# Twelve adaLN reductions taken out of the first FFN and placed in the mixer, eleven of them from the keys' projection on

## The chip, the core and the metric

The kernel is one launch on one core of a Trainium2 chip (trn2). The metric is device time in microseconds (us), taken as the median of several runs. All sizes are float32: one layer of a model of width 2048, 256 tokens, batch 1. The engines are called as the profile calls them: PE (TensorE, matrix products), PEld (its weight loads), DVE (VectorE), ACT (ScalarE), POOL (GpSimd) and SP (SyncE, which here only issues the large DMA transfers).

## The reference, cut to what matters

The layer is two half-step feed-forward blocks (FFN) around a mixer. Each of the three sublayers is modulated: its input is shifted and scaled, and its output is gated, by vectors that come from one large matrix `w_ada` and a single conditioning vector `c`.

```python
mod = (jax.nn.silu(c) @ w_ada[l] + b_ada[l]).reshape(B, N_SUBLAYERS, 3, D_MODEL)
shift, scale, gate = mod[:, :, 0], mod[:, :, 1], mod[:, :, 2]
y = _swiglu(modulate(x, 0), ffn1_w13[l], ffn1_w2[l])
x = _layer_norm(ALPHA * x + FFN_WEIGHT * gate[:, 0, None, :] * y, ln_g[l, 0], ln_b[l, 0])
proj = modulate(x, 1) @ w_in[l] + b_in[l]
q, k, v, o, i_pre, f_pre, x_rg, g_rg = jnp.split(proj, ...)
...                                   # mLSTM heads on q, k, v; RG-LRU on x_rg, g_rg
y = jnp.concatenate([h_m, h_r], axis=-1) @ w_out[l]
x = _layer_norm(ALPHA * x + gate[:, 1, None, :] * y, ln_g[l, 1], ln_b[l, 1])
y = _swiglu(modulate(x, 2), ffn2_w13[l], ffn2_w2[l])
x = _layer_norm(ALPHA * x + FFN_WEIGHT * gate[:, 2, None, :] * y, ln_g[l, 2], ln_b[l, 2])
```

`silu(c) @ w_ada` has 3 x 3 x 2048 outputs, and each is a dot product of length 2048. These outputs are the "adaLN tiles" of the title: 128 outputs to a tile, 144 tiles. They depend on `c` alone, so that a tile can be computed at any time before the sublayer that uses it.

## The kernel before, in words

**Weights.** All weights are read once, in tiles of 128 x 2048 float32 (1 MB each). `load` (line 77) takes a buffer with `raw_tile` (line 68, four buffers in all, one tag "raw") and issues the transfer on SP's queue. `split` (line 84) makes two halves of a tile for PE: ACT casts it to a rounded high part (line 91), DVE subtracts that from the raw tile to give the low part (line 93). High and low parts have three buffers each ("hi" and "lo"). Each product is then taken as high x high, low x high and high x low: lines 252 to 254 in `mov_t` and lines 241 and 243 in `stat_u`. In the profile's names a raw tile begins with r, its high part with h and its low part with l: `rs`, `hs`, `ls` belong to one tile of the `w_s` projections, `rv`, `hv`, `lv` to the values, `rwo`, `hwo`, `lwo` to the output projection, `rw`, `rfg` and `rfv` to the FFNs.

**adaLN tiles.** `ada_tile` (line 166) takes the next tile of the list `todo`, loads it into one of the same four raw buffers, and lets DVE reduce it against a broadcast of silu(c) in one instruction (line 175), with a short instruction behind it that writes the 128 sums. PE and ACT have no part in it. The tiles are spread by a credit: each `load` calls `tick` (line 183), which adds a rate to a counter and issues one adaLN tile for each whole unit:

```python
credit[0] += credit[1]
while todo and credit[0] >= 1.0:
    credit[0] -= 1.0
    ada_tile()
```

The rate is set at the beginning of each stage: `RAMP_RATE` for the first five stages, `FFN1_RATE` at line 835, `MIX_RATE` at line 933 in `mixer`, `FFN2_RATE` at line 839. `ada_until` (line 178) issues in one go what a stage needs and hasn't got yet; with the rates before and after the change only line 1162 may find anything left to do.

**PSUM.** All products go to eight banks of 128 x 512 float32 (`bank`, line 65). A bank is free again when its last reader on ACT or DVE is done.

**Order.** The instructions of a stage are written in program order, but a scheduler of the framework sets the order on each engine from its own estimate of the times, and it also decides which buffer and which bank a tile takes. On the chip each engine then works through its own list strictly in that order and waits on semaphores. So a change in the number of DVE instructions changes all engines' lists.

**The mixer** (line 899), in the order of its program: the output gate's projection; the input and forget gates; eight tiles for the RG-LRU's input (line 1045) with the convolution; eight for its gelu gate (line 1049) with the recurrence (line 1013) and `rg_out` (line 1030, DVE instructions on 128 x 512); the values in two groups of four tiles, two banks per group (lines 1057 to 1067: the products go to `pv`, and DVE adds the bias and moves them out at line 1065); eight tiles of keys (line 1069: `pj`, moved out by ACT at line 916 and DVE at line 917); eight of queries, two to a head. Between the heads' queries PE takes up the attention of the heads before: `head` (line 1073) forms masks from `pm` on DVE (lines 1078 and 1080), ACT's exponential (line 1082), and the weighted scores from `pk` on DVE (line 1089, in place in `misc`); `head_out` (line 1092) multiplies them with the values into `pn` and normalises that on DVE and POOL (lines 1100 to 1115). The last two heads stand between the tiles of the output projection (`out_tile`, line 1132, products into `pw`); `head_split` (line 1117) transposes their results, and the mixer ends with a boundary that leads to the second FFN.

## Time and profile before

| | |
|---|---|
| median of 3 runs | 1914.12 us (1912.11 to 1915.27) |
| the profiled execution: its own time | 1910.49 us |
| the profiled execution: its span | 1908.7 us |
| DVE busy in the span | 1434.7 us (75%) |
| ACT busy in the span | 835.3 us (44%) |
| mean granted clock of PE | 0.996 |

The profiled execution is a fourth run beside the three; its span is counted from its first to its last instruction, and the 1.8 us between that and its own time lie around the span.

How the work lies in the span (a view by windows, DVE's adaLN instructions taken alone in the last column):

| stretch, us from the start | stage | PE busy | DVE busy | DMA rate | adaLN on DVE |
|---|---|---|---|---|---|
| 307 to 745 | first FFN behind the ramp | 435.31 of 438 | 364.68 | 350 GB/s | 140.72 us |
| 824 to 968 | mixer, RG-LRU and values | 143.69 of 144 | 137.12 | 291 GB/s | 30.36 us |
| 968 to 1035 | keys and the first queries | 67.00 of 67 | 52.72 | 309 GB/s | 14.15 us |
| 1035 to 1110 | heads and output projection | 75.00 of 75 | 60.37 | 231 GB/s | 14.06 us |

A row of the lists below reads: start or line, duration, engine, line of the kernel, operation, output and inputs, shape, and how many instructions are merged in it ("x4"); in brackets stands how long the engine was idle ahead of it and who ended that. A DVE instruction overlaps the next by a little, so that what it costs in a row of work is the distance from its start to the next one's. The clock is the share of full speed that was granted to PE in a window.

### The profile page before, as it was taken

To read this page: it belongs to the slowest core of one execution; us is meant where nothing else is said; L and a number is where in the kernel's file an instruction comes from. 1 tells how busy PE (TensorE), PEld (TensorE's weight loads), DVE (VectorE), ACT (ScalarE), POOL (GpSimd) and SP (SyncE) were. 2 spreads that over 40 slices of the span, in tenths; PEclk is the share of its full clock that TensorE was granted. 3 is DMA by queue.
4 is the path that set the end of the run, shared out by engine and by line. 5 is a ranking of instruction groups with operands and counts; after the bars stand their busy time and mean duration, and the time that the engine had idled before them with its cause. 6 is when DMAs were issued, how large, how long until landed. Compare 5 with 4: busy or idle time off the path is not lost.

```text
span 1908.7 us, 21186 instructions
## 1 busy us (share of the span) xinstructions
PE 1868.9 (98%) x8551; PEld 1543.8 (81%) x8551; DVE 1434.7 (75%) x1394; ACT 835.3 (44%) x788; POOL 39.5 (2%) x65
## 2 busy tenths in 40 slices
PE   6999999999999999999999999999999999999997
PEld 5778888888887888688888887888888888888886
DVE  7999898888887977889996887555555644545676
ACT  5434344533333335756644356443444333333341
POOL 0000000000000000100000121000000000000000
PEclk9999999999999999999999999999999999999999
DMA  9999888999999987477687563676666655555552
GB/s 370 345 344 346 319 301 346 348 364 359 346 353 358 354 326 264 151 271 293 252 321 288 207 260 131 241 264 224 261 240 247 240 195 182 196 193 205 198 220 88
DMA packets 73203, 515.88 MB, mean 270 GB/s; under 512 B 8544, under 2 KB 8720, under 8 KB 11024
## 3 DMA queue, kind: packets, MB, share of 16 engines
q1 hardware_dynamic: 70848, 507.54, 71.0%
q10 hardware_dynamic: 1728, 3.80, 0.6%
q0 software_dynamic: 528, 3.17, 0.4%
q8 instruction: 67, 1.10, 0.2%
q14 instruction: 32, 0.26, 0.0%
HBM read 512.36 MB, written 2.12 MB: 270 GB/s over the span
## 4 chain that ended last, share of the span: by engine, by line
PE 88%; DVE 5%; DMA 3%; ACT 2%; issue 2%; POOL 0%; DVEq 0%; ACTq 0%; POOLq 0%
PE py L253 6%; PE py L254 6%; PE py L252 6%; PE fg L253 6%; PE fg L254 6%; PE fg L252 6%; PE pj L241 5%; PE fv L253 5%; PE fv L254 5%; PE fv L252 5%; PE pj L243 3%; PE tl L252 2%; PE tl L253 2%; PE tl L254 2%; PE rg L685 2%
## 5 line engine op out<-in xcount | busy, mean ns | idle before, releaser
L175 DVE CUSTOM_DVE_ANT_0 ada<-ada,scb,badac 128x2048 f32<-128x2048 f32 x142 | 332.7, 2345 | 7.1 <-DMA ada<-in_w_ada 7.0
L93 DVE TENSOR_TENSOR lw<-rw,hw 128x2048 fp32r<-128x2048 f32 x81 | 185.2, 2288 | 96.8 <-ACT hw L91 96.8
L91 ACT CAST hw<-rw 128x2048 fp32r<-128x2048 f32 x81 | 155.0, 1913 | 226.3 <-PE py L254 68.1
L93 DVE TENSOR_TENSOR lfv<-rfv,hfv 128x2048 fp32r<-128x2048 f32 x60 | 137.5, 2292 | 129.5 <-ACT hfv L91 129.3
L93 DVE TENSOR_TENSOR lfg<-rfg,hfg 128x2048 fp32r<-128x2048 f32 x60 | 137.4, 2290 | 92.9 <-ACT hfg L91 92.9
L253 PE MATMUL py<-lw,hth 128*128 128x512 f32 x512 | 200.3, 391 | 2.6 <-DVE lw L93 2.5
L254 PE MATMUL py<-hw,htl 128*128 128x512 f32 x512 | 200.0, 391 | 0.0
L91 ACT CAST hfg<-rfg 128x2048 fp32r<-128x2048 f32 x60 | 114.9, 1915 | 190.3 <-PE fv L254 55.9
L252 PE MATMUL py<-hw,hth 128*128 128x512 f32 x512 | 196.9, 393 | 0.0
L253 PE MATMUL fg<-lfg,u 128*128 128x512 f32 x480 | 187.0, 389 | 0.1
L254 PE MATMUL fg<-hfg,u 128*128 128x512 f32 x480 | 187.0, 389 | 0.0
L253 PE MATMUL fv<-lfv,u 128*128 128x512 f32 x480 | 186.8, 389 | 0.0
L91 ACT CAST hfv<-rfv 128x2048 fp32r<-128x2048 f32 x60 | 114.7, 1912 | 164.5 <-PE fg L254 91.7
L254 PE MATMUL fv<-hfv,u 128*128 128x512 f32 x480 | 186.7, 389 | 0.0
L252 PE MATMUL fg<-hfg,u 128*128 128x512 f32 x480 | 185.0, 392 | 0.0
L252 PE MATMUL fv<-hfv,u 128*128 128x512 f32 x480 | 183.5, 389 | 0.0
L91 ACT CAST hra<-rra 128x2048 fp32r<-128x2048 f32 x47 | 89.9, 1915 | 133.6 <-PE rv L686 50.6
L241 PE MATMUL pj<-u,hs 128*128 128x512 f32 x512 | 122.5, 391 | 0.0
L253 PEld LDWEIGHTS py<-lw,hth 128*128 128x128 f32 x512 | 96.6, 189 | 23.6 <-DVE lw L93 3.9
L93 DVE TENSOR_TENSOR lra<-rra,hra 128x2048 fp32r<-128x2048 f32 x47 | 107.3, 2285 | 9.3 <-ACT hra L91 9.1
L254 PEld LDWEIGHTS py<-hw,htl 128*128 128x128 f32 x512 | 96.5, 189 | 20.1
L252 PEld LDWEIGHTS py<-hw,hth 128*128 128x128 f32 x512 | 96.1, 188 | 19.5
(445 smaller groups left out, 3470.7 us busy)
## 6 DMA issues: line engine op xcount, KB each, us to landing
ada<-in_w_ada SPq DMA_DIRECT2D x144, 1024.0 KB, 5.5
rw<-in_w SPq DMA_DIRECT2D x81, 1024.0 KB, 4.9
rfg<-in_w SPq DMA_DIRECT2D x60, 1024.0 KB, 4.9
rfv<-in_w SPq DMA_DIRECT2D x60, 1024.0 KB, 4.8
rra<-in_w_r SPq DMA_DIRECT2D x48, 1024.0 KB, 5.5
rs<-in_w_s SPq DMA_DIRECT2D x32, 1024.0 KB, 4.8
rwo<-in_w_out SPq DMA_DIRECT2D x16, 1024.0 KB, 4.8
rv<-in_w_vo SPq DMA_DIRECT2D x8, 1024.0 KB, 4.9
```

Of the source, the lines that this page charges most:

```text
L91: act.copy(cut(hi, w), like(raw[:, w], hi))
L93: low.tensor_sub(cut(lo, w), like(raw[:, w], lo), cut(hi, w).bitcast(F32))
L175: vec.tensor_tensor_reduce(raw[:, c], raw[:, c], scb[:, c], 1.0, base, ALU.mult, ALU.add, to)
L241: nc.tensor.matmul(ps, hi[:, k * P:(k + 1) * P], both(k), start=k == 0, stop=False)
L243: nc.tensor.matmul(ps[:, 0:S], lo[:, k * P:(k + 1) * P], uh[:, k, :], start=False, stop=k == KT - 1)
L252: nc.tensor.matmul(o, acth[:, k0 + j, tk], cut(hi, w), start=first and j == 0, stop=False)
L253: nc.tensor.matmul(o, acth[:, k0 + j, tk], cut(lo, w), start=False, stop=False)
L254: end = nc.tensor.matmul(o, actl[:, k0 + j, tk], cut(hi, w), start=False, stop=last and j == 3)
L685: nc.tensor.matmul(pss[t], uh[:, k0 + j, tk], lo[:, w], start=False, stop=False)
```

## The change

Two rates change, and one of them gets a second value that holds from the keys' projection on.

```diff
-FFN1_RATE = 0.88
-MIX_RATE = 0.5
+FFN1_RATE = 0.72
+MIX_RATE = (0.55, 1.05)
...
-                credit[:] = -2.0, MIX_RATE
+                credit[:] = -2.0, MIX_RATE[0]
...
         kt_ = v8(slot("k"))
+        credit[1] = MIX_RATE[1]
         proj(17, 8, kt_)
```

No instruction is added or removed; 144 adaLN tiles are issued as before. Counted in SP's list of transfers:

| stage | loads of weights | adaLN tiles before | after |
|---|---|---|---|
| ramp | | 40 | 40 |
| first FFN behind it | 72 | 63 | 51 |
| mixer, up to the keys | | 11 | 12 |
| mixer, from the keys on | 24 that may bring one | 14 | 25 |
| second FFN | | 16 | 16 |

The scheduler then orders all lists anew from the first FFN on. From line 1069 on, line numbers of the kernel are higher by one after the change (DVE's line 1089 is 1090, and so on). Three places are shown.

**DVE, behind the values and ahead of line 1065.** The L1065 rows move the values out of their four banks; L93 on `ls` is the low part of a tile of the keys, L175 an adaLN reduction, the `t`, `rl` rows the end of `rg_out`. Before, with the third tile of the keys (`ls_6870`) just ahead of the four rows:

```order
L175 ISA ada_6908,adac<-ada_6908,scb,badac 128x2048
L175 ISA adac 128x1
L1040 SCALAR_TENSOR_TENSOR t_6490<-t_6490,xc 128x512
L1037 TENSOR_TENSOR t_6499<-t_6499,gg 128x512
L93 TENSOR_TENSOR ls_6829<-rs_6826,hs_6828 128x2048
L1042 TENSOR_TENSOR rl<-t_6490,rh 128x512
L1039 SCALAR_TENSOR_TENSOR t_6499<-t_6499,gg 128x512
L93 TENSOR_TENSOR ls_6870<-rs_6867,hs_6869 128x2048
L1040 SCALAR_TENSOR_TENSOR t_6499<-t_6499,xc 128x512
L1065 TENSOR_TENSOR v<-pv_6515,bv_6517 128x2x256
L1065 TENSOR_TENSOR v<-pv_6516,bv_6517 128x2x256
```

After it, with the sixth tile of the keys (`ls_6975`) ahead of them:

```order
L93 TENSOR_TENSOR ls_6931<-rs_6928,hs_6930 128x2048
L175 ISA ada_6969,adac<-ada_6969,scb,badac 128x2048
L175 ISA adac 128x1
L1039 SCALAR_TENSOR_TENSOR t_6463<-t_6463,gg 128x512
L1042 TENSOR_TENSOR rl<-t_6454,rh 128x512
L93 TENSOR_TENSOR ls_6975<-rs_6972,hs_6974 128x2048
L175 ISA ada_7013,adac<-ada_7013,scb,badac 128x2048
L175 ISA adac 128x1
L1040 SCALAR_TENSOR_TENSOR t_6463<-t_6463,xc 128x512
L1065 TENSOR_TENSOR v<-pv_6479,bv_6481 128x2x256
L1065 TENSOR_TENSOR v<-pv_6480,bv_6481 128x2x256
```

Between the low part of the last gelu-gate tile (line 93, `ls_6433` before and `ls_6397` after) and the first L1065 row, DVE's list has 12 rows of line 93 and 5 adaLN reductions before, and 15 and 10 after.

**PE, the fourth, fifth and sixth tile of the keys**, with the semaphores that a row waits for. Before:

```order
L241 MATMUL pj_6907<-u_105,hs_6913 128x512 [waits Activation_49]
L241 MATMUL pj_6907<-u_105,hs_6913 128x512 x15
L243 MATMUL pj_6907<-u_105,ls_6914 128x256 [waits DVE_49]
L243 MATMUL pj_6907<-u_105,ls_6914 128x256 x15
L241 MATMUL pj_6951<-u_105,hs_6954 128x512 [waits Activation_49]
L241 MATMUL pj_6951<-u_105,hs_6954 128x512 x15
```

After:

```order
L241 MATMUL pj_6880<-u_105,hs_6886 128x512 [waits Activation_49]
L241 MATMUL pj_6880<-u_105,hs_6886 128x512 x15
L243 MATMUL pj_6880<-u_105,ls_6887 128x256 [waits DVE_49]
L243 MATMUL pj_6880<-u_105,ls_6887 128x256 x15
L241 MATMUL pj_6924<-u_105,hs_6930 128x512 [waits DVE_49,Activation_49]
L241 MATMUL pj_6924<-u_105,hs_6930 128x512 x15
```

The fifth tile's product (`pj_6924`) now waits for DVE ahead of its first matmul: the value of that semaphore in the built program is the one that the first L1065 row raises, since the tile takes the bank of `pv_6479`. The sixth to eighth tile wait in the same way for the other three L1065 rows.

**PE, the last two heads** (`pn_7700` before, `pn_7697` after is the first product of head 3 with the values, `pn_7614` and `pn_7633` are those of head 2; `pm` and `pk` are head 3's mask and scores; `pw` is the output projection). Before, right behind head 2's two products:

```order
L1077 MATMUL pm_7656<-misc,ident 128x256
L1085 MATMUL pk_7661<-qt_7449,k 128x256 x2
L1087 MATMUL pk_7661<-qt_7449,k 128x128 x2
L253 MATMUL pw_7586<-lwo_7673,rh 128x512
L254 MATMUL pw_7586<-hwo_7672,rl 128x512
L252 MATMUL pw_7586<-hwo_7672,rh 128x512
L253 MATMUL pw_7586<-lwo_7673,rh 128x512
L254 MATMUL pw_7586<-hwo_7672,rl 128x512
L252 MATMUL pw_7586<-hwo_7672,rh 128x512
L253 MATMUL pw_7586<-lwo_7673,rh 128x512
L254 MATMUL pw_7586<-hwo_7672,rl 128x512
L1097 MATMUL pn_7700<-v,misc 128x257
```

After:

```order
L1098 MATMUL pn_7614<-v,misc 128x257
L1098 MATMUL pn_7633<-v,misc 128x257 x2
L1078 MATMUL pm_7653<-misc,ident 128x256
L1086 MATMUL pk_7658<-qt_7440,k 128x256 x2
L1088 MATMUL pk_7658<-qt_7440,k 128x128 x2
L1098 MATMUL pn_7697<-v,misc 128x257
L1098 MATMUL pn_7716<-v,misc 128x257 x2
L252 MATMUL pw_7736<-hwo_7743,rh 128x512
```

Before, eight matmuls of the output projection stand between head 3's scores and its product with the values; after it they stand ahead of `pn_7614`, and none is left between. `pn_7697` waits for the last of these DVE rows, which follow in DVE's list after the change upon line 1101 of `pn_7633`:

```order
L175 ISA ada_7865,adac<-ada_7865,scb,badac 128x2048
L175 ISA adac 128x1
L1079 SCALAR_TENSOR_TENSOR misc<-pm_7653,gcol,misc 128x256
L1081 SCALAR_TENSOR_TENSOR misc<-pm_7653,gcol,misc 128x128
L93 TENSOR_TENSOR lwo_7838<-rwo_7835,hwo_7837 128x2048
L1103 TENSOR_TENSOR rd_7616<-rd_7616,pn_7614 128x1
L1115 TENSOR_SCALAR pn_7529<-pn_7529,hmv_7537,rsh_7543 128x256
L1106 BN_STATS hst_7620<-pn_7614 128x6
L1103 TENSOR_TENSOR rd_7636<-rd_7636,pn_7633 128x1
L1106 BN_STATS hst_7640<-pn_7633 128x6
L1113 TENSOR_TENSOR rsh_7563<-rsh_7563,rd_7551 128x1
L1090 SCALAR_TENSOR_TENSOR misc<-pk_7658,misc 128x384
```

Before, the two mask rows and the row of the scores (`L1078`, `L1080`, `L1089` for head 3) have five short rows between them, with no tile's low part and no adaLN reduction among them.

## The prediction

> **What bounds the kernel now.** I read the page's first lines first, then the list of PE's own waits, then windows around the one that lies in the first FFN.

> ```profile
> span 1908.7 us, 21186 instructions
> PE 1868.9 (98%) x8551; PEld 1543.8 (81%) x8551; DVE 1434.7 (75%) x1394; ACT 835.3 (44%) x788; POOL 39.5 (2%) x65
> PE py L253 <- DVE lw L93: 2.5, 1, 2.5
> PE tu L116 <- DVE n L116: 3.9, 3, 2.3
> PE pv L253 <- DVE lv L93: 0.3, 1, 0.3
> ```

> PE is busy for 98% of the span, so the time is PE's work plus what PE waits. An adaLN tile costs PE nothing where it stands; what it costs is DVE time and a transfer, and it reaches the end only where PE then waits for a late DVE or DMA. So the question is where PE waits, before and after. Between 600 and 1200 us the list has one wait in the first FFN (`py`, 2.5 us), the boundary's (`tu`, which the change doesn't touch), and 0.3 us in the values.

> ```profile
> 604.84 8.55 DMA rw<-in_w
> 605.00:610.00 5.00, 5.00 (x24) 4.14 (x23) 2.36 (x2) 1.47 (x1) 0.00 (x0) 1.00 1.02 429
> 610.00:615.00 5.00, 3.28 (x15) 2.39 (x13) 2.82 (x3) 1.95 (x2) 0.00 (x0) 1.00 0.95 398
> 615.00:620.00 5.00, 4.19 (x12) 3.33 (x13) 5.00 (x4) 2.28 (x2) 0.00 (x0) 0.66 0.62 216
> 620.00:625.00 5.00, 5.00 (x24) 4.12 (x23) 4.70 (x4) 0.65 (x1) 0.00 (x0) 1.00 0.99 382
> 1170.00:1175.00 5.00, 3.39 (x8) 1.14 (x6) 3.05 (x11) 4.18 (x11) 0.70 (x2) 1.00 0.75 277
> ```

> The chain shows the wait in the first FFN: one weight tile took 8.55 us to land, with the DMA engines full (share 1.02). In the windows PE has 1.72 us idle at 610 to 615 and 0.81 at 615 to 620, and then the granted clock falls to 0.66 of full speed over 5 us, which is 5.00 x 0.34 = 1.7 us of work lost. So this stall costs 2.5 + 1.7 = 4.2 us. An idle stretch of 1.6 us (1170 to 1175) kept the clock at 1.00.

> **What the change takes away.** In the first FFN 12 of 63 adaLN tiles go: per weight tile there come 1 + 51/72 = 1.71 transfers of 1 MB in place of 1 + 63/72 = 1.88, 9% fewer, and the four raw buffers are shared by fewer tiles. That is where the 8.55 us came from, so I take the stall as gone: -4.2 us. Bounds: 0 (the stall comes at another place) to -4.2; PE's list of waits in that stage has nothing else to give, at least in this execution.

> **What it adds in the mixer.** First the prices, start to start, on DVE:

> ```profile
> 985.40 0.42 DVE L917 TENSOR_TENSOR k<-k,pj 128x256 f32<-128x256 f32 x1
> 985.73 2.29 DVE L93 TENSOR_TENSOR ls<-rs,hs 128x2048 fp32r<-128x2048 f32 x1
> 987.94 0.42 DVE L917 TENSOR_TENSOR k<-k,pj 128x256 f32<-128x256 f32 x1
> 988.27 2.35 DVE L175 CUSTOM_DVE_ANT_0 ada<-ada,scb,badac 128x2048 f32<-128x2048 f32 x1
> 990.54 0.09 DVE L175 DVE_READ_ACCUMULATOR2_ANT adac<- 128x1 f32 x1
> 990.54 2.29 DVE L93 TENSOR_TENSOR ls<-rs,hs 128x2048 fp32r<-128x2048 f32 x1
> ```

> A low part costs 2.20, an adaLN reduction 2.27, an L917 row 0.33. Averaged over the stage there would be room: by the table ahead DVE is idle for 67 - 52.7 = 14.3 us from 968 to 1035 and 75 - 60.4 = 14.6 us from 1035 to 1110, together 28.9 us, against 11 x 2.27 = 25.0 us added. But the lists are strict, so I follow two places where PE waits for a definite row.

> *The fifth tile of the keys.* After the change it needs the bank that the first L1065 row frees. The rows that time this:

> ```profile
> 913.63 2.29 DVE L93 TENSOR_TENSOR ls<-rs,hs 128x2048 fp32r<-128x2048 f32 x1 [1.53 <-ACT hs L91]
> 920.00:930.00 10.00, 10.00 (x54) 8.60 (x53) 10.00 (x12) 6.91 (x8) 1.25 (x3) 1.00 0.79 292
> 975.40 2.48 DVE L1065 TENSOR_TENSOR v<-pv,bv 128x512 f32<-128x512 f32 x4
> 980.00:990.00 10.00, 10.00 (x61) 8.88 (x60) 10.00 (x10) 3.98 (x3) 0.00 (x0) 1.00 0.84 328
> 984.68 3.65 PE pj L241 x16
> 988.33 1.91 PE pj L243 x16
> 990.24 3.65 PE pj L241 x16
> ```

> Before, DVE went from the last gelu-gate tile (913.63) to L1065 (975.40) in 61.8 us, and was idle in none of it that matters: in the windows (the fourth number of a row is DVE's busy time) it is busy for all of the 10 us, from 920 to 990. So its time there is the sum of its rows. After the change the same stretch has three more low parts (3 x 2.20 = 6.6), five more reductions (5 x 2.27 = 11.35) and some short rows that the scheduler put earlier (three of 512 columns and a few small ones, about 1.9): 19.8 us more, hence L1065 at 913.6 + 81.6 = 995.2, and its first row, 0.6 us, ends at 995.8. The start is held by ACT's cast and the same work of PE as before, so it stays within about 1 us. PE came to the fifth tile at 990.24. It will be there at the latest 995.8 - 990.2 = 5.5 us behind before, and I take 5.2, allowing DVE a slightly earlier start. Part of this PE may already wait for the fourth value tile's low part, which also moves back by 2.27 and the scan ahead of it; that wait lies inside the 5.2. Bounds: 3 us if DVE starts 2 us earlier, 8 if a raw tile lands late and DVE idles.

> *Head 3.* DVE has caught up with PE before it (with 15 us idle in 1035 to 1110 it waits for `pn` and `pm` rows), so I count from the end of head 2's second `pn` product.

> ```profile
> 1053.73 0.48 DVE L1078 SCALAR_TENSOR_TENSOR misc<-pm,gcol,misc 128x256 f32<-128x256 f32 x1
> 1054.12 0.34 DVE L1080 SCALAR_TENSOR_TENSOR misc<-pm,gcol,misc 128x128 f32<-128x128 f32 x1
> 1054.38 0.14 DVE L1102 TENSOR_TENSOR rd<-rd,pn 128x1 f32<-128x1 f32 x1
> 1054.44 0.42 DVE L1105 BATCH_NORM_STATS2 hst<-pn 128x6 f32<-128x256 f32 x1
> 1055.37 0.53 DVE L1089 SCALAR_TENSOR_TENSOR misc<-pk,misc 128x384 f32<-128x384 f32 x1
> 1060.33 1.00 DVE L1114 TENSOR_SCALAR pn<-pn,hmv,rsh 128x256 f32<-128x256 f32 x2
> 1061.24 0.74 DVE L1115 TENSOR_TENSOR og<-og,pn 128x256 f32<-128x256 f32 x2
> 1075.46 1.46 PE L1097 MATMUL pn<-v,misc 128*128 128x257 f32 x6
> 1076.85 0.69 PE L1077 MATMUL pm<-misc,ident 4*128 4x256 f32 x2
> 1078.44 0.61 PE L1087 MATMUL pk<-qt,k 128*128 128x128 f32 x4
> 1078.81 0.47 PE L253 MATMUL pw<-lwo,rh 128*128 128x512 f32 x1
> 1080.74 1.46 PE L1097 MATMUL pn<-v,misc 128*128 128x257 f32 x6
> ```

> On DVE, after the change: line 1101's short row 0.13, the reduction 2.27, the masks 0.39 + 0.26, the low part 2.20, then 2 x 0.06 + 0.46 + 2 x 0.34 + 0.06 = 1.3, then the scores' row 0.46 to 0.53: 7.1 us. PE meanwhile does `pm` and `pk`, 1076.85 to 1078.81, 2.0 us, and has nothing else in its list: it waits 5.1 us. Before, it had eight matmuls there and DVE's scores came in time (`pn` at 1080.74 with PE never idle). Directly behind, `pw` (`pw_7736`) takes the bank of `pn_7529`, which an L1116 row frees that stands behind one more reduction: 2.27 + 0.06 + 0.33 = 2.7 us from the scores, against 1.3 us of PE's three products: 1.3 us more. Together 6.4 us. Bounds: 2.8 (were the reduction and the low part both hidden by an earlier DVE, since masks, exponential and scores must follow PE's `pm` in any case: 7.1 - 2.27 - 2.0) to 9 (DVE 2.6 us late, the price of one more reduction).

> *The clock.* The row of 615 to 620 shows 1.7 us lost after 2.5 us idle, and 1.6 us idle cost none. Both new stalls exceed 2.5 us, so 1.7 each: 3.4 (0 to 3.4). [...]

> Hidden, and taken at nothing: the twelfth tile, ahead of the keys, for DVE's low parts lead PE there by several us (without that cover 2.3 us); the transfers, since DVE's pace of a low part and a reduction leaves each of four raw buffers two such pairs, 2 x (2.20 + 2.27) = 8.9 us, for a landing of 4.8 (the page's median for these tiles, quoted below); the last four reductions, behind head 3, for which ten us of `pw` matmuls are on PE's list.

> **Sum.** -4.2 + 5.2 + 6.4 + 3.4 = +10.8 us against the profiled execution's own time of 1910.49 us (span 1908.7 us): 1921.3 us. The median of the runs shown is 1914.12 us, 3.6 above the profiled one, and no row says where those lie; where they are more stalls like that of the first FFN, the change removes them. I let half of them stay: 1921.3 + 1.8 = 1923 us.

> **The rivals.**

> *The clock holds.* The stalls come in pieces, each below 2.5 us, or fall so that the clock is not lowered. For it: one case of each kind is all the trace has. Against it: 5.1 us is twice the idle that sufficed. 1923 - 3.4 = 1919.6 us.

> *The transfers become the limit.* From the keys on a weight tile (3.65 + 1.91 = 5.56 us of PE) comes with 1.05 adaLN tiles: 2.05 x 1.0486 MB in 5.56 us is 387 GB/s.

> ```profile
> rs<-in_w_s SPq DMA_DIRECT2D x32, 1024.0 KB, 4.8
> 0.00:50.00 50.00, 32.65 (x136) 26.49 (x136) 37.70 (x42) 25.72 (x35) 3.33 (x11) 0.93 0.94 371
> 400.00:450.00 50.00, 50.00 (x224) 41.39 (x223) 38.64 (x28) 18.81 (x12) 0.00 (x0) 1.00 0.95 364
> ```

> No 50 us of the trace hold more than 371 GB/s. At 364 a tile takes 5.9 us, 0.35 us more, over the 16 tiles of keys and queries 5.6 us: 1928.5 us. Against it: DVE paces these transfers below that rate, and the heads give PE 1.3 to 3.4 us more per two tiles.

> *The first FFN was dearer than the profile says* (the other side). Mechanism: a raw tile that lands late with full DMA engines, 4.2 us each time. If the timed runs have three such stalls rather than one, 1914.1 + 15.0 - 12.6 = 1916.5 us, which can't be told from no change; from four on (16.8) the change is faster than before, 1912 us or less. For it: 3.6 us of the median are unexplained, about one stall more. Against it: that makes two, not four.

> **How the numbers follow.** The forecast has 0.60, the clock's rival 0.15, the transfers 0.13, the first FFN's 0.12 (0.08 near no change, 0.04 faster). A change under 0.2%, 3.8 us, can't be told from none: 1910.3 to 1917.9. A few of the forecast's cases with both bounds low (3 + 2.8) fall there as well, so faster 0.04, same 0.11, slower 0.85. The range takes the bounds of both stalls around 1923, down to the clock's rival and a little below, and most of the transfers': 1917 to 1929.

> **What would show it.** In PE's list of waits after: `pj` L241 on DVE `v` L1065 (with `pv` on `lv` ahead of it) adding up to about 5 us near 990; `pn` L1098 on DVE `misc` L1090 near 5; `pw` L252 on `og` L1116 near 1.3; `py` on `lw` gone. DVE idle nowhere from 920 to 995. The clock below 1.00 in a window near 1000 and one near 1090, and not near 615. Wrong would be: L1065 before 990 (then DVE's list had slack that I don't see), PE busy across `pn_7697`, or waits for DMA among the keys.

## The result, and the profile after

| | before | after |
|---|---|---|
| median, runs beside each other | 1913.53 us (6 runs, 1912.11 to 1915.27) | 1923.28 us (6 runs, 1921.88 to 1924.50) |
| ratio after / before | | 1.0051, 95% interval 1.0040 to 1.0062 |
| profiled execution: span | 1908.7 us | 1921.3 us |
| mean granted clock of PE | 0.996 | 0.991 |

The change makes the kernel slower by 9.8 us, or 7.7 to 11.9 us. Where the profiled execution lost it is found by following the same matmul of PE through both traces:

| PE comes to | before, us | after, us | after less before |
|---|---|---|---|
| `py`, first product of the first FFN's second half | 301.83 | 303.63 | +1.80 |
| `pif`, start of the mixer | 824.00 | 822.81 | -1.19 |
| `pr`, gates of the RG-LRU | 894.39 | 893.21 | -1.18 |
| `pcol`, behind the keys | 1012.44 | 1017.44 | +5.00 |
| `pm` of head 0 | 1035.24 | 1040.24 | +5.00 |
| `f`, the boundary | 1160.19 | 1172.77 | +12.58 |

So the ramp, which the change doesn't touch, took 1.8 us more in this execution; the first FFN gave 3.0 us; the values and keys cost 6.2; the last two heads 7.6; nothing changed behind them (12.6 at the end of the span). Without the ramp that is -3.0 + 6.2 + 7.6 = +10.8 us.

PE's list of waits in the changed kernel, from 300 to 1130 us (what PE waited for, total us, times, longest):

```profile
PE pn L1098 <- DVE misc L1090: 5.2, 1, 5.2
PE pj L241 <- ACT rh L1041: 2.5, 1, 2.5
PE pv L253 <- DVE lv L93: 2.2, 1, 2.2
...
PE fg L253 <- DVE lfg L93: 1.2, 1, 1.2
PE fv L253 <- DVE lfv L93: 0.6, 1, 0.6
```

The 2.5 us at `py` are gone from the first FFN, and two smaller waits, 1.2 and 0.6, are there in its place. Three waits of the mixer are new. The rows around them, from the timeline of the changed kernel (the values, then the keys, then head 3):

```profile
912.45 2.27 DVE L93 TENSOR_TENSOR ls<-rs,hs 128x2048 fp32r<-128x2048 f32 x1
...
933.18 4.41 DVE L1027 TENSOR_TENSOR_SCAN xc<-xr,ii 128x2048 f32<-128x2048 f32 x1
937.52 2.31 DVE L175 CUSTOM_DVE_ANT_0 ada<-ada,scb,badac 128x2048 f32<-128x2048 f32 x1
939.77 2.27 DVE L93 TENSOR_TENSOR lv<-rv,hv 128x2048 fp32r<-128x2048 f32 x1
942.10 0.77 PE L253 MATMUL pv<-lv,u 128*128 128x512 f32 x1 [2.17 <-DVE lv L93]
...
991.32 2.34 DVE L175 CUSTOM_DVE_ANT_0 ada<-ada,scb,badac 128x2048 f32<-128x2048 f32 x1
994.19 2.48 DVE L1065 TENSOR_TENSOR v<-pv,bv 128x512 f32<-128x512 f32 x4
995.02 3.88 PE L241 MATMUL pj<-u,hs 128*128 128x512 f32 x16 [2.48 <-ACT rh L1041]
...
1083.99 2.34 DVE L175 CUSTOM_DVE_ANT_0 ada<-ada,scb,badac 128x2048 f32<-128x2048 f32 x1
1086.26 0.48 DVE L1079 SCALAR_TENSOR_TENSOR misc<-pm,gcol,misc 128x256 f32<-128x256 f32 x1
1086.91 2.28 DVE L93 TENSOR_TENSOR lwo<-rwo,hwo 128x2048 fp32r<-128x2048 f32 x1
1090.42 0.55 DVE L1090 SCALAR_TENSOR_TENSOR misc<-pk,misc 128x384 f32<-128x384 f32 x1
1091.03 2.94 PE L1098 MATMUL pn<-v,misc 128*128 128x257 f32 x6 [5.16 <-DVE misc L1090]
1093.24 0.40 DVE L1116 TENSOR_TENSOR og<-og,pn 128x256 f32<-128x256 f32 x1
1093.78 0.77 PE L252 MATMUL pw<-hwo,rh 128*128 128x512 f32 x1
```

In the values a reduction and a scan of 4.4 us stand ahead of the fourth tile's low part, and PE is 2.17 us early. At the fifth tile of the keys PE waits 2.48 us. The list names an ACT cast there, which ended at 994.92 us; it is a cast of the recurrence's output (`rh`), which this product doesn't read. The cast of the tile's own high part was done at 991.49 + 1.91 = 993.40, and the first of the four merged L1065 rows ended at 994.19 + 0.68 = 994.87, just ahead of PE's start. In the run of three reductions less, below, the same wait is put down to L1065 itself. At head 3 DVE goes through a reduction and a low part while PE waits for the scores. The matmul of 0.77 us at 942.10, twice the usual 0.39, shows that the clock had been lowered; windows of 3.41 us, the shortest stretch at one clock in this trace, cut at the clock's own steps, show when (third number PE busy, then PEld, DVE, ACT, POOL, the granted clock, the DMA share and GB/s):

```profile
938.80:942.21 3.41, 1.24 (x6) 0.70 (x5) 3.41 (x4) 3.13 (x2) 0.00 (x0) 0.99 0.38 79
942.21:945.62 3.41, 3.41 (x8) 2.68 (x9) 3.41 (x4) 0.69 (x2) 0.00 (x0) 0.51 1.01 423
...
989.99:993.40 3.41, 2.55 (x19) 2.24 (x17) 3.41 (x2) 1.91 (x1) 0.00 (x0) 1.00 0.88 332
993.40:996.81 3.41, 1.79 (x8) 1.54 (x9) 3.41 (x8) 2.09 (x5) 0.00 (x0) 1.00 0.99 401
...
1085.57:1088.98 3.41, 0.29 (x3) 0.10 (x1) 3.41 (x5) 0.52 (x1) 1.19 (x1) 0.99 0.95 327
1088.98:1092.39 3.41, 1.36 (x3) 1.18 (x4) 3.41 (x9) 0.00 (x0) 0.00 (x0) 0.50 1.02 389
1092.39:1095.81 3.42, 3.42 (x9) 2.35 (x8) 3.42 (x16) 0.00 (x0) 1.13 (x4) 0.51 0.64 211
```

Half clock (0.51 and 0.50 in these rows) for 3.41 us costs 3.41 x 0.5 = 1.7 us of PE's work where PE is busy throughout. It came behind the 2.17 us in the values, not behind the 2.48 us at the fifth tile, whose idle time falls into two windows (PE busy 2.55 and 1.79 us), and twice at head 3, where PE idled for 3.41 - 1.36 = 2.05 us of the first half-clock window anyway: (6.83 - 2.05) / 2 = 2.4 us lost. With that the stages add up: 2.17 + 1.7 + 2.48 less the 0.3 of before is 6.1 (6.2 measured), and 5.16 + 2.4 is 7.6 (7.6 measured).

### The profile page after: what moved, and what is told of

Read it like the earlier page. It is cut to its first block, busy times and chain, and to the rows that moved or that the text cites. A ratio compares the mean times of both kernels' runs of the same rounds, so it can differ in the third digit from the quotient of the medians.

```text
span 1921.3 us, 21178 instructions
## 1 busy us (share of the span) xinstructions
PE 1874.5 (98%) x8551; PEld 1548.1 (81%) x8551; DVE 1434.2 (75%) x1394; ACT 833.7 (43%) x788; POOL 46.0 (2%) x65
## 4 chain that ended last, share of the span: by engine, by line
PE 78%; DVE 8%; DMA 7%; issue 4%; ACT 2%; POOL 0%; DVEq 0%; ACTq 0%; POOLq 0%
DMA ada<-in_w_ada 6%; PE fg L253 5%; PE fg L254 5%; PE fg L252 5%; PE fv L254 5%; PE fv L253 5%; PE fv L252 5%; PE pj L241 5%; PE py L254 5%; PE py L252 5%; PE py L253 5%; PE pj L243 2%; PE tl L252 2%; PE tl L253 2%; PE tl L254 2%
## 5 line engine op out<-in xcount | busy, mean ns | idle before, releaser
L175 DVE CUSTOM_DVE_ANT_0 ada<-ada,scb,badac 128x2048 f32<-128x2048 f32 x142 | 332.7, 2345 | 66.5 <-DMA ada<-in_w_ada 66.4
L91 ACT CAST hw<-rw 128x2048 fp32r<-128x2048 f32 x81 | 155.0, 1914 | 243.5 <-PE py L254 106.7
L93 DVE TENSOR_TENSOR lw<-rw,hw 128x2048 fp32r<-128x2048 f32 x81 | 185.2, 2289 | 98.1 <-ACT hw L91 98.1
L93 DVE TENSOR_TENSOR lfv<-rfv,hfv 128x2048 fp32r<-128x2048 f32 x60 | 137.3, 2291 | 119.5 <-ACT hfv L91 119.5
L93 DVE TENSOR_TENSOR lfg<-rfg,hfg 128x2048 fp32r<-128x2048 f32 x60 | 137.3, 2290 | 88.8 <-ACT hfg L91 88.8
L91 ACT CAST hfg<-rfg 128x2048 fp32r<-128x2048 f32 x60 | 114.9, 1914 | 200.8 <-PE fv L254 69.1
L252 PE MATMUL py<-hw,hth 128*128 128x512 f32 x512 | 200.1, 392 | 0.0
L253 PE MATMUL py<-lw,hth 128*128 128x512 f32 x512 | 199.1, 389 | 0.0
L91 ACT CAST hfv<-rfv 128x2048 fp32r<-128x2048 f32 x60 | 114.8, 1913 | 182.6 <-PE fg L254 128.4
L252 PE MATMUL fg<-hfg,u 128*128 128x512 f32 x480 | 188.1, 392 | 0.0
L253 PE MATMUL fg<-lfg,u 128*128 128x512 f32 x480 | 187.0, 389 | 1.2 <-DVE lfg L93 1.2
L253 PE MATMUL fv<-lfv,u 128*128 128x512 f32 x480 | 186.8, 389 | 0.6 <-DVE lfv L93 0.6
L252 PE MATMUL fv<-hfv,u 128*128 128x512 f32 x480 | 186.4, 389 | 0.0
L91 ACT CAST hra<-rra 128x2048 fp32r<-128x2048 f32 x47 | 89.9, 1914 | 131.1 <-PE rv L686 46.2
L241 PE MATMUL pj<-u,hs 128*128 128x512 f32 x512 | 122.6, 391 | 2.5 <-ACT rh L1041 2.5
L93 DVE TENSOR_TENSOR lra<-rra,hra 128x2048 fp32r<-128x2048 f32 x47 | 107.3, 2284 | 8.9 <-ACT hra L91 8.9
L252 PEld LDWEIGHTS py<-hw,hth 128*128 128x128 f32 x512 | 96.1, 188 | 19.6
L253 PEld LDWEIGHTS py<-lw,hth 128*128 128x128 f32 x512 | 96.2, 188 | 19.4
## 6 DMA issues: line engine op xcount, KB each, us to landing
ada<-in_w_ada SPq DMA_DIRECT2D x144, 1024.0 KB, 5.6
rw<-in_w SPq DMA_DIRECT2D x81, 1024.0 KB, 5.0
rfg<-in_w SPq DMA_DIRECT2D x60, 1024.0 KB, 5.0
rfv<-in_w SPq DMA_DIRECT2D x60, 1024.0 KB, 4.9
rra<-in_w_r SPq DMA_DIRECT2D x48, 1024.0 KB, 5.3
rs<-in_w_s SPq DMA_DIRECT2D x32, 1024.0 KB, 5.1
rwo<-in_w_out SPq DMA_DIRECT2D x16, 1024.0 KB, 4.8
rv<-in_w_vo SPq DMA_DIRECT2D x8, 1024.0 KB, 4.8
```

Source lines behind the costliest of these rows:

```text
L91: act.copy(cut(hi, w), like(raw[:, w], hi))
L93: low.tensor_sub(cut(lo, w), like(raw[:, w], lo), cut(hi, w).bitcast(F32))
L175: vec.tensor_tensor_reduce(raw[:, c], raw[:, c], scb[:, c], 1.0, base, ALU.mult, ALU.add, to)
L241: nc.tensor.matmul(ps, hi[:, k * P:(k + 1) * P], both(k), start=k == 0, stop=False)
L252: nc.tensor.matmul(o, acth[:, k0 + j, tk], cut(hi, w), start=first and j == 0, stop=False)
L253: nc.tensor.matmul(o, acth[:, k0 + j, tk], cut(lo, w), start=False, stop=False)
```

## The experiments

Times in us are ratios times the median of before in the same session (1913.05 to 1914.35). The change itself stands at +9.8 (7.7 to 11.9).

**The two halves apart.** The first FFN's part, with the 12 tiles that leave it not computed:

```diff
-MIX_RATE = (0.55, 1.05)
+MIX_RATE = (0.5, 0.5)
...
+    nc.gpsimd.memset(adac, 0.0)
-    todo = list(enumerate(_ada_tiles()))
+    todo = [(i, t) for i, t in enumerate(_ada_tiles()) if not (t[0] == 2 and t[1] < 2 and 3 <= t[2] < 9)]
```

> The first FFN's part alone: FFN1_RATE 0.72, the mixer at its old rate of 0.5, and the 12 tiles that leave the first FFN are not computed at all (shift and scale of the last sublayer, kt 3 to 8, stay zero). The built lists of the mixer are then those of before. Theory (the change is a sum of stalls): only the first FFN's stalls change. In the two traces that stage lost 4.2 us before and 1.2 us net after it, so 3.0 us less than before: 1910.5 us (1909 to 1912). Rival 1 (the stall is rare, the timed runs of before don't have it): 1913.5 us. Rival 2 (the timed runs have several such stalls): 1908 us or less.

Measured 1907.72 us, ratio 0.9972 (0.9962 to 0.9983): -5.4 us (-7.3 to -3.3). Rival 1 falls; the time is below the theory's 1909 to 1912 and at the bound of rival 2, and the interval holds both. In its trace the list shows no wait of the first FFN from 300 us on, where the changed kernel's had 1.8 us of small ones. From the first `py` to `pif` PE takes 819.58 - 303.11 = 516.5 us, against 522.2 in the trace of before and 519.2 in that of the change: 5.7 us less than before, which is what the timed runs show. Of the 5.7, 4.2 are the stall at `py` with its clock; the other 1.5 went in pieces of 0.1 to 0.3 us at low parts that came a little late, too short for the list of waits. So one stall and these small pieces suffice for the timed 5.4 us, and no second stall is needed.

The mixer's part, with FFN1_RATE at 0.88 and those 12 tiles computed twice:

```diff
-FFN1_RATE = 0.72
+FFN1_RATE = 0.88
...
-    todo = list(enumerate(_ada_tiles()))
+    todo = [(i, t) for i, t in enumerate(_ada_tiles())
+            for _ in range(2 if t[0] == 2 and t[1] < 2 and 3 <= t[2] < 9 else 1)]
```

> The mixer's part alone: FFN1_RATE 0.88 as before, the mixer with the change's rates, and 12 adaLN tiles computed twice so that the mixer has as many as after the change (its built lists are the change's). Theory: the waits near the values, at the fifth tile of the keys and at head 3 stay, which in the changed kernel's trace are worth 6.2 us up to the fifth tile and 7.6 us at head 3 with the clock: 1913.5 + 13.8 = 1927.3 us (1925 to 1929). Rival (the first FFN's part gives nothing, the mixer's is the whole difference): 1923.3 us. Together with the first FFN's part alone it should add up to the change's +9.8 us.

Measured 1926.56 us, ratio 1.0073 (1.0056 to 1.0091): +14.0 us (10.7 to 17.4), as the theory had it. The two parts add to +8.6, the change has +9.8. The same waits are in its trace, with the first FFN's back:

```profile
PE pn L1099 <- DVE misc L1091: 5.2, 1, 5.2
...
PE py L254 <- DVE lw L93: 2.5, 1, 2.5
PE pj L242 <- ACT rh L1042: 2.5, 1, 2.5
...
PE pv L254 <- DVE lv L93: 2.2, 1, 2.2
```

**DVE or the transfers.** Of the 25 tiles from the keys on, 11 (every second one of the first 22) are only reduced, without a transfer:

```diff
+        late[0] += late[1]
+        odd = late[0] > 0 and late[0] % 2 == 0 and late[0] <= 22
+        if not odd:
+            nc.sync.dma_start(raw, a["w_ada"][i])
...
-            vec.tensor_tensor_reduce(raw[:, c], raw[:, c], scb[:, c], 1.0, base, ALU.mult, ALU.add, to)
+            vec.tensor_tensor_reduce(raw[:, c], (scb if odd else raw)[:, c], scb[:, c], 1.0, base, ALU.mult, ALU.add, to)
...
         credit[1] = MIX_RATE[1]
+        late[1] = 1
```

> The change, but 11 of the 25 tiles from the keys on bring no transfer: their reduction reads the broadcast of silu(c) in place of the tile (those 11 outputs are then wrong). The transfers are as many as before, DVE's work is the change's. In the built list one reduction more stands ahead of line 1065 than in the change (11 for 10), and head 3 has the same rows. Theory (DVE's list is late): the stalls stay, the fifth tile's is 2.3 us longer: 1925.5 us (1922 to 1929). Rival (the transfers are the limit): the stalls from the keys on go, 1909.5 to 1913 us.

Measured 1931.2 us, ratio 1.0089 (1.0071 to 1.0108): +17.0 us, above the theory's 1922 to 1929 and far from the rival's 1909.5 to 1913. The stalls stay without the transfers; the fifth tile's is 3.2 us longer for the one more reduction (2.3 expected), and its idle time of 5.7 us brought two windows at half clock (a granted clock of 0.82 from 995 to 1000 us and of 0.50 from 1000 to 1005), 2.9 us of PE's work, which the change's 2.5 us had not:

```profile
PE pj L246 <- ACT rh L1046: 5.7, 1, 5.7
PE pn L1104 <- DVE misc L1096: 5.2, 1, 5.2
```

The same 11 only transferred and not reduced (with `adac` zeroed at the start, and `return` behind the transfer where `odd` holds):

> The change, but 11 of the 25 tiles from the keys on are only transferred and not reduced (those 11 outputs stay zero). The transfers are the change's, DVE's work is that of before. In the built list line 1065 stands behind the fourth tile of the keys, and head 3 has its eight matmuls of the output projection again. Theory (DVE's list is late): the stalls at the fifth tile and at head 3 go, the one in the values (2.2 us and 1.7 us of clock) stays: 1910.5 + 3.9 = 1914.4 us (1911 to 1916). Rival (the transfers are the limit): 1921 to 1924 us.

Measured 1912.42 us, ratio 1.0002 (0.9990 to 1.0015): no change, inside the theory's 1911 to 1916 us. The fifth tile's wait is gone, head 3's is down to 1.6 us:

```profile
PE pv L260 <- DVE lv L93: 2.2, 1, 2.2
PE pn L1106 <- DVE misc L1098: 1.6, 1, 1.6
```

So DVE's reductions make the stalls of the change, not its transfers. Whether by their time alone or by the order that the scheduler makes of them, this run can't tell, since in its lists line 1065 stood behind the fourth tile of the keys and head 3 had its eight matmuls again; the next four runs hold the order and keep the reductions.

**Can the order be mended?** Two orders are held by an edge: DVE's rows for the fifth tile of the keys and later ones behind L1065 (first edit), and the output projection's second tile on PE behind head 3's scores (second edit).

```diff
+                with ExitStack() as stack:
+                    if i0 + i >= 21:
+                        stack.enter_context(tc.issue_after(moved[0].ins))
+                    w = load_w(a["w_s"][i0 + i], f"s{i0 + i}")
-                nc.vector.tensor_add(v[:, t, 2 * n:2 * n + 2, 0:DH],
+                moved[0] = nc.vector.tensor_add(v[:, t, 2 * n:2 * n + 2, 0:DH],
```

```diff
-        out_tile(0, 3, False, False)
+        with tc.issue_after(score[0].ins):
+            out_tile(0, 3, False, False)
```

> The change, with one order held: DVE does the four rows of line 1065 ahead of the low parts (and reductions) of the fifth tile of the keys and all behind it. In the built list ten low parts less one... read as: line 1065 stands behind the fourth tile of the keys with 8 reductions ahead, in place of the sixth with 10. Theory (PE waits at the fifth tile for that row alone): the 2.5 us that PE waited there go and nothing takes their place, the stall in the values and head 3 stay: 1922.8 - 2.5 = 1920.3 us (1918.5 to 1921.5). Rival (DVE as a whole is late, the low parts that now come later are waited for): 1922 to 1924 us.

Measured 1929.31 us, ratio 1.0084 (1.0071 to 1.0097): +16.1 us, dearer than the change and than both theories. The fifth tile's wait did go, L1065 came at 980.85. But the scheduler laid out everything behind it anew, and at 1044.64 us PE waits for a tile of the queries, with a longer stall at the heads (first the waits, then the timeline):

```profile
PE pw L252 <- DVE og L1122: 6.0, 1, 6.0
PE pn L1104 <- DVE misc L1096: 5.2, 1, 5.2
PE pj L241 <- ACT hs L91: 2.4, 1, 2.4
```

```profile
1036.68 2.34 DVE L175 CUSTOM_DVE_ANT_0 ada<-ada,scb,badac 128x2048 f32<-128x2048 f32 x1
...
1039.06 0.33 SPq L81 DMA_DIRECT2D rs<-in_w_s  x1
...
1042.70 3.70 ACT L91 CAST hs<-rs 128x2048 fp32r<-128x2048 f32 x2
...
1044.64 1.77 PE L241 MATMUL pj<-u,hs 128*128 128x512 f32 x4 [2.35 <-ACT hs L91]
```

The weight tile's transfer is issued at 1039.06, just when DVE has finished a reduction (1036.68 + 2.34 = 1039.02) and its raw buffer is free, and ACT can cast it 3.6 us later: a late reduction holds back a weight tile through the four shared buffers.

> The change, with one order held: PE does all 24 matmuls of the output projection's second tile behind head 3's scores, so that they stand between those and the product with the values. Theory (head 3's stall is DVE's reduction and low part with nothing on PE's list to cover them): 7.6 us go, 5.2 of waiting, 3.4 of clock less 1.0 for what PE has to do anyway: 1922.8 - 7.6 = 1915.2 us (1913.5 to 1917.5). Rival (DVE is late as a whole and PE meets it a few matmuls later): 1920 us or more.

Measured 1921.54 us, ratio 1.0046 (1.0032 to 1.0059): +8.8 us (6.1 to 11.3), which can't be told from the change's +9.8; the expected 7.6 us did not come. The one wait of 5.2 us became five, none longer than 1.6 us:

```profile
PE pn L1100 <- DVE misc L1092: 2.1, 2, 1.3
PE pw L252 <- ACT u L1129: 1.6, 1, 1.6
PE pw L253 <- DVE lwo L93: 1.1, 1, 1.1
```

With 0.3 us at `pt` they are 5.1 us together, and none lowered the clock (granted 1.00 from 945 to 1180 us). From `pcol` to `f` PE takes 154.2 us in this trace, 155.3 in the change's and 147.8 in that of before. Here matmuls between the scores and the product did not cover a DVE that was behind; PE met it a little earlier and a little later.

> The change with both orders held (line 1065 ahead of the fifth tile, the output projection's matmuls behind head 3's scores). Theory: the two savings add, and the stall in the values (2.2 us and 1.7 us of clock) stays: 1922.8 - 2.5 - 7.6 = 1912.7 us (1911 to 1914.5). Rival: they don't add, 1916 us or more.

Measured 1927.97 us, ratio 1.0074 (1.0062 to 1.0086): +14.2 us. The first edit's stall at the queries and 8.4 us of waits at the heads are in its trace. The savings don't add; the rival held. The 2.2 us in the values are there too, but this time no half clock came behind them (granted 1.00 from 900 to 1045 us).

> As the run with both orders held, and the mixer's rates are 0.5 and 1.1 in place of 0.55 and 1.05: the mixer has 11 tiles up to the keys, as before, and 26 from there on. Theory (the twelfth tile ahead of the keys makes the values' fourth tile late): that stall goes too, 1912.7 - 3.9 = 1908.8 us (1907 to 1910.5), which is the first FFN's part alone (1907.7 us), faster than both kernels. Rival (it only moves to another place, or one tile more behind the keys makes a new wait): 1911 us or more.

Measured 1921.24 us, ratio 1.0048 (1.0036 to 1.0061): +9.2 us; again the rival. The wait in the values did go, as expected (0.3 us left, as before), but head 3 then waits 7.4 us in two pieces and the output projection 2.3 us. No order that was tried brings the gain back.

**How many tiles, and where.** Half the move (FFN1_RATE 0.8, MIX_RATE 0.5 and 0.8):

> Half of the move: FFN1_RATE 0.8 (57 tiles) and mixer rates 0.5 and 0.8, that is 11 tiles up to the keys and 20 from there on. In the built lists line 1065 stands behind the fourth tile of the keys with two reductions more than before, and PE has its eight matmuls between head 3's scores and its product again. Theory (the stalls come from the amount of DVE work between rows that PE waits for, past a slack): no stall of over 1 us in the mixer: 1910 us (1908 to 1912). Rival (each tile moved costs the same, 13.5 us over 12 tiles): 1913.1 - 2.7 + 6.8 = 1917 us.

Measured 1915.11 us, ratio 1.0003 (0.9994 to 1.0012): +0.6 us, above the theory's 1908 to 1912 and below the rival. Up to the heads PE's waits are those of the kernel before, but head 3 still stalls:

```profile
1078.22 0.47 DVE L1079 SCALAR_TENSOR_TENSOR misc<-pm,gcol,misc 128x256 f32<-128x256 f32 x1
...
1078.87 2.34 DVE L175 CUSTOM_DVE_ANT_0 ada<-ada,scb,badac 128x2048 f32<-128x2048 f32 x1
...
1081.78 2.29 DVE L93 TENSOR_TENSOR lwo<-rwo,hwo 128x2048 fp32r<-128x2048 f32 x1
1083.98 0.55 DVE L1090 SCALAR_TENSOR_TENSOR misc<-pk,misc 128x384 f32<-128x384 f32 x1
1084.59 2.94 PE L1098 MATMUL pn<-v,misc 128*128 128x257 f32 x6 [4.83 <-DVE misc L1090]
```

A reduction and a low part stand between the masks and the scores again, and eight matmuls on PE (1.8 us) don't cover them. So one reduction and one low part in the wrong place were enough for nearly the whole stall of the change (4.83 of 5.16 us); the cost is not one price per tile.

The same half, placed by hand: 11 tiles with the first 13 loads, 2 in the next 6, 4 in the next 5, 3 behind line 1162.

```diff
+        if plan:
+            credit[0] = plan.pop(0)
...
+        plan.extend([0, 1, 0, 1] + [1] * 4 + [1] * 5 + [0] + [0, 0, 1, 0, 1] + [1, 1, 0, 1, 1] + [1, 1, 1, 0])
...
-        ada_until(2, 1, KT - 1)
-        credit[:] = 0.0, 0.0
         for i, k in enumerate((2, 3, 0, 1)):
             out_tile(2, k, i == 0, i == 3)
+        ada_until(2, 1, KT - 1)
+        credit[:] = 0.0, 0.0
```

> The same half of the move, but the 20 tiles from the keys on are placed by hand: 11 with the first 13 loads, 2 with the next 6 (the heads, where DVE has the least room), 4 with the next 5 and 3 with the loads behind line 1162, which bring none in either kernel. Theory: as for the half move, without what is left of waits at the heads: 1909 us (1907 to 1911). Rival (placement doesn't matter): the same time as the half move within 1 us. Rival (the loads behind line 1162 make the boundary late): 1913 us or more.

Measured 1913.58 us, ratio 0.9994 (0.9986 to 1.0003): -1.1 us, not told from no change, and above the theory's 1907 to 1911. `pn` waits 0.3 us, but two waits of the output projection (1.6 and 2.0 us) follow at 1092 and 1096, and a half-clock window behind the second (granted clock 0.68 over the 5 us from 1095). From `pcol` to `f` PE takes 154.1 us, 155.1 in the half move and 147.8 before, so the stall at the heads has moved and not gone. The boundary, which the second rival had late, waits as in all runs.

Three reductions less, the last three ahead of head 3's scores, out of the change's eleven:

```diff
+        late[0] += late[1]
+        if 21 <= late[0] <= 23:
+            return
```

> The change, but three of its 25 tiles from the keys on (numbers 21 to 23, the last three reductions ahead of head 3's scores) are only transferred, not reduced (their outputs stay zero). The built lists are the change's up to the values and the keys. Theory (head 3's stall is made by the few reductions that stand between the rows that head 3 hands from DVE to PE and back): 5.2 us of waiting and 3.4 us of clock go, the stalls in the values and at the fifth tile stay: 1922.8 - 8.6 = 1914.2 us (1912.5 to 1916). Rival (all eleven have made DVE late by then, three less leave most of it): two thirds or more of the 8.6 us stay, 1919.5 us or more.

In its trace the waits from 820 to 1130 us are these two; head 3's is gone:

```profile
PE pj L247 <- DVE v L1071: 2.7, 1, 2.7
PE pv L259 <- DVE lv L93: 2.2, 1, 2.2
```

The time says it less clearly: 1919.24 us, ratio 1.0030 (1.0015 to 1.0045), 4.1 us better than the change where 7.6 should go, and 10 runs that spread from 1913.48 to 1925.28 us (those of before beside them from 1910.23 to 1918.54). The trace tells more than the time: from `pcol` to `f` PE takes 1166.84 - 1018.94 = 147.9 us, against 155.3 in the change's trace and 147.8 in that of before, so 7.4 us are gone at the heads. In that execution the ramp, which has the same lists on PE and DVE, took 4.0 us more than in the change's, the first FFN 2.7 us less and the boundary 1.7 us more. So leaving three of the eleven reductions out removes the whole of head 3's stall in the profiled execution; part of that may be the order, for with them gone no low part stands between the masks and the scores either, and four matmuls stand on PE behind the scores. That it is worth 7.6 us in the median is not shown.

**A place that has room.** The first FFN's last eight loads bring no tile in either kernel. Six of the 63 tiles go there, none to the mixer:

```diff
-FFN1_RATE = 0.72
-MIX_RATE = (0.55, 1.05)
+FFN1_RATE = 0.8
+MIX_RATE = (0.5, 0.5)
...
-                credit[:] = 0.0, 0.0
+                credit[:] = 0.2, 0.75
                 g2_kept(gi - 1)
```

> No tile goes to the mixer: FFN1_RATE 0.8 gives the first 72 loads 57 adaLN tiles in place of 63, the other 6 go with the last 8 loads of the first FFN (its last products, about 700 to 745 us), which bring none in either kernel; the mixer's rate and built lists are those of before. The trace of before has 279 GB/s in that stretch and DVE idle for 16.8 of 45 us. Theory (the first FFN's stall comes from too many transfers per weight tile in its first 72 loads): most of the 5.3 us of the first FFN's part alone are had, and the mixer costs nothing: 1909 us (1907.5 to 1911). Rival 1 (57 tiles are still too many): 1912 to 1914 us. Rival 2 (the tail's tiles make the boundary behind it late): 1914 us or more.

Measured 1909.14 us, ratio 0.9968 (0.9956 to 0.9981): 6.1 us faster than before (3.6 to 8.4) and faster than the change (1.0051). The stretch from 690 to 745 us, first before, then with the six tiles (same columns as above):

```profile
690.00:745.00 55.00, 55.00 (x248) 45.57 (x247) 36.21 (x33) 27.62 (x29) 0.00 (x0) 1.00 0.79 296
```

```profile
690.00:745.00 55.00, 55.00 (x248) 45.57 (x247) 47.03 (x41) 25.61 (x26) 0.00 (x0) 1.00 0.95 360
```

DVE has 10.8 us more to do and the DMA engines 64 GB/s more to move, PE is busy for all 55 us as before, and its waits in the mixer are those of before. The time lies in the theory's range of 1907.5 to 1911 us. This is the version to keep.

## Why the prediction was right, step by step

**The first FFN, -4.2.** Right in mechanism; in size the traces give 3.0 us in the change, where small waits are left, and 5.7 in the part alone. At 0.88 tiles per load both traces (before, and the mixer's part alone) have the 2.5 us wait with its half clock (granted 0.51 from 615.57 to 618.98 us in before, 0.50 from 617.0 to 620.3 in the part); at 0.80 three traces of three have 0.1 us or less; at 0.72 six of nine have none, and three have 0.8 to 2.4 us, though PE's and DVE's lists of that stage are the same in all nine. So the stall is made rarer, not impossible. Timed, the part is worth 5.4 us (3.3 to 7.3); that the list of waits had "nothing else to give" missed 1.5 us of small pieces.

**The fifth tile, 5.2.** Right. The count of rows gave 81.6 us from the gelu gate's last low part to L1065; it took 994.19 - 912.45 = 81.74. PE's wait came in two pieces, as allowed for, 2.17 us in the values and 2.48 at the tile, 4.65 together, about half a microsecond less than said. But that the twelfth tile ahead of the keys costs nothing was wrong: at a rate of 0.5 instead of 0.55 the scan of 4.4 us doesn't stand ahead of the fourth value tile's low part, and 0.3 us are left of the 2.17.

**Head 3, 6.4.** The first term, 5.1, was 5.16. The second, 1.3 us for `pw`, did not occur: at half clock PE's products took 1093.78 - 1091.03 = 2.75 us instead of 1.3, and the L1116 row was done at 1093.64.

**The sum.** -4.2 + 5.2 + 6.4 + 3.4 = +10.8 stood in the forecast, and -3.0 + 6.2 + 7.6 = +10.8 in the traces, so the terms' errors (first FFN 1.2 too much, the two mixer places 0.7 and 0.5 too much) cancel. That they cancel to the tenth is luck. The median moved by 9.8, where 1923 against 1914.1 was +8.9. The step from the profile to the median, "half of them stay", had no good ground. The traces offer another place for the 3.6 us than more stalls of the first FFN: PE comes to the first `py` at 301.8 us in the profile of before, the earliest of all 14 traces, and at 302.3 to 309.5 us in the others (median of all 303.9), with the same lists on PE and DVE up to there; and the boundary behind the mixer took 1.7 us more in nine of the 14, but not in before (last section). Neither is touched by the change, so that by them the whole 3.6 us should have stayed. That the timed runs of before lost their time there is not shown, since only one execution of before has a trace.

**The rivals.** The transfers are refuted by the two runs on DVE and DMA, the first FFN being dearer by its part alone (5.4 us, and not the 12.6 of three stalls or the 16.8 of four that the rival needed), the clock that holds by the windows (granted clock 0.51 from 942.21, 0.50 from 1088.98).

**What the averages hid.** The prediction set aside 28.9 us of idle DVE against 25.0 us added, and the runs show why that was right: from 1035 to 1110 us, where DVE idles for 14.6 us before, the half move already stalls PE for 4.8 us. Of its six more tiles, two fall in this stretch: 18.8 us of adaLN on DVE in place of 14.1. DVE's idle time there is spent between rows that PE hands it one by one, and a reduction of 2.27 us that doesn't fit such a gap delays the next row.

## What to carry to other kernels

Here background work on an engine with 20% idle time (DVE from 1035 to 1110 us before: 14.6 of 75) was free only where nothing waited for its next row. Ask of each stage how long the engine can be late before the other waits, not how busy it is: the first FFN's tail took six reductions and PE stayed busy for all 55 us, the heads stalled for 4.8 us with one reduction and one low part between two rows that PE needed. Where a stall came from the amount of work ahead of a row, holding an order moved it to another place in all four runs that tried; moving the work to another stage removed it.

## What the runs showed of the hardware

The clock's grid puts a step of 1.7 us on the time: in these traces, whether a stall of 2 to 3 us cost that on top went with where it fell in a window of 3.41 us (2.17 us in the values did, 2.48 us at the fifth tile did not), and so differed between traces with the same stall. The boundary behind the mixer shows it. In all 14 traces PE waits 2.3 us there, yet from the first `f` of that boundary to the first `fg` behind it PE takes 52.6 us in five of them and 54.1 to 54.3 us in nine. The wait's window and the next, first in before, then in the first FFN's part alone:

```profile
1172.00:1175.41 3.41, 1.39 (x4) 0.32 (x2) 1.39 (x6) 2.96 (x10) 0.74 (x2) 1.00 0.93 382
1175.41:1178.83 3.42, 3.16 (x17) 2.15 (x18) 2.92 (x6) 3.23 (x7) 0.00 (x0) 1.00 0.36 151
```

```profile
1168.06:1171.47 3.41, 1.11 (x5) 0.28 (x4) 1.39 (x6) 2.96 (x9) 0.74 (x2) 1.00 1.00 387
1171.47:1174.88 3.41, 3.41 (x12) 2.27 (x12) 2.47 (x5) 2.93 (x8) 0.00 (x0) 0.50 0.26 103
```

Before has 2.02 us of the wait in the one window and the rest in the next, and keeps its clock (1.00); the other has all 2.3 us in one window and loses half of the next (0.50). The ramp differs as well: its first 60 us, with the same lists, have a mean clock of 0.94 in before and 0.86 after. That is 3.6 and 8.4 us at the rate of lost clock, about two and five half-clock windows; part of it falls into waits, since the ramp was 1.8 us longer and not 4.8. An effect of 2 us in one profile of this kernel may be no more than that.
